# A decoder layer on one Trainium2 core: the products of the conditioning vector with its weights on TensorE instead of VectorE

## The chip, the core and the metric

The kernel runs on one core of one Trainium2 chip. The core has TensorE (PE; its weight loads are shown apart as PEld), VectorE (DVE), ScalarE (ACT), GpSimd (POOL) and SyncE (SP), which here issues nearly all DMA transfers. The metric is the time of one execution on the device in microseconds (us). Three runs of the kernel before took 1175.67, 1179.12 and 1177.77 us; the median is 1177.77.

## What is computed

One layer over 1024 tokens of width 1024, all in float32. A conditioning vector c gives six vectors of length 1024: three for the mixing half (shift, scale, gate 1), three for the MLP half. They are numbered s = 0 to 5, in the order in which the reference splits them: sh1, sc1, g1, sh2, sc2, g2.

```python
c_act = jax.nn.silu(c)                                  # (1, 1024)
mod = c_act @ w_ada + b_ada                             # w_ada: (1024, 6 * 1024)
sh1, sc1, g1, sh2, sc2, g2 = split(mod, 6)
h = rmsnorm(x, pre_mix_g) * (1 + sc1) + sh1
q, k, v, u = split(h @ w_in)                            # 512, 128, 128, 512 columns
attn = sliding_window_attention(q, k, v, attn_sinks)    # window of 128, ALiBi, sinks
ssm = s5_mixer(u, ...)                                  # 32 groups, 64 complex states each, a scan over the tokens
mixed = concat(rmsnorm(attn, ...), rmsnorm(ssm, ...)) @ w_out
x = x + g1 * rmsnorm(mixed, post_mix_g)
h = rmsnorm(x, pre_mlp_g) * (1 + sc2) + sh2
x = x + g2 * rmsnorm(square(relu(h @ w_mlp_in)) @ w_mlp_out, post_mlp_g)
```

The change concerns the second line alone: a vector of 1024 times a matrix of 1024 x 6144 (24 MB in float32).

## The kernel before

The kernel is written with a framework that orders the instructions of each engine itself, by priorities and its own model of time, and sets all waits. Buffers are slots with a name: a new tile in a slot waits until every reader of the tile before it is done. `pin` (line 124) keeps the DMAs that are given to it in the order of the program. Only in the MLP is TensorE's order written out by hand (from line 1345). Each engine works through its queue in order. SyncE's queue is such a queue too: a load that waits for its slot holds up what is issued behind it.

**The vector c.** `cact` (lines 166 to 169) holds silu(c) as 128 x 8: row p of column q is element 128 q + p. A product of c with a block of w_ada is made in two steps. First DVE multiplies the eight row blocks of w_ada (128 rows each) by the columns of cact and adds them up, eight operations in a chain; this leaves a sum for each partition. Then TensorE adds over the 128 partitions, by a product with a tile of ones. A float32 product takes two records in the trace. The slot names that matter: S0 to S3, S6, S7 and G2S hold loaded weights, G1S the sums, PSUM bank D (one bank) the products.

**Shift and scale 1 (lines 368 to 414).** The loop runs over the eight chunks k of the width. `load_k` (line 130) loads the columns of w_ada for shift and scale of chunk k, as four transfers of 256 KB with rows of 512 bytes, three chunks ahead (lines 368, 369, 376). Two chains of four (line 390 on ACT, line 392 on DVE) make the sums `acc`, one addition joins them, and line 397 adds over the partitions into `aps`; lines 399 and 400 make sh1 and G1 of the chunk. With these `h_step(k, 0)` turns the normalised tokens of the first half (transposes `xt`, line 362) into h, as two parts `h1h` and `h1l`, and `u_step` multiplies them with the weights of u (lines 85 to 87, three products each). Beside it run the parameters of the state space model on GpSimd and DVE (`params0` to `params2`, `f_group`).

**Shift and scale 2, gate 1 (lines 417 to 474, 507).** `ada_acc` (line 419) makes a sum `macc` over a whole vector: eight loads `adm` of 512 KB (128 rows of 4 KB) into the ring of four slots RAWS, and eight operations on DVE, 128 x 1024 each (lines 425 and 427). `mods2` makes shift and scale 2 from two such sums (eight products into `mp` each, line 440). `gate` makes gate 1: it adds the bias in one row (line 453), adds over the partitions and copies to all of them in one product with ones (`gp`, line 459), multiplies by the gain of the norm (line 460) and copies the result into slot G1S (line 461), where it stays until the output projection. These steps are taken by `bg_steps`, between the steps of the tokens' second half (lines 479 to 490).

**The scan.** When all of u is there, it is transposed (`ut`, line 498) and multiplied by F (`vp`, line 503); then DVE runs the scan over chunks of tokens (tiles `st`, `Vs`, `qw`, lines 510 to 544), which needs slots G2S and S7 of the ring, and a correction (lines 594 to 608). Beside it run the q, k and v projections (line 617 on; six column blocks m, each with loads `wr`, splits into two parts `whi` on ACT and `wlo` on DVE, and products `pq`), and tables on GpSimd (`Gs`, line 564). The product `kp` (line 575) is the one place where four small products stand side by side in the column groups of the array.

**Output projection (lines 952 to 1004).** For each of eight token tiles j: products `po` (lines 943 to 946), evictions `mix` (lines 948, 950), the residual with gate 1 (`mix` times `macc`, line 967), norm, transposes `x2t` and h of the MLP. Two steps of gate 5 are taken ahead of each tile from the second on (line 993), with a single slot S0 for the loads; the finished gate 5 is stored to DRAM (`g2d`, line 1004) and read again at the end of the MLP (line 1314).

**MLP (line 1005 on).** Products on TensorE, from about 480 us to the end; the change leaves it as it is, but for the name of the DRAM tile that line 1314 reads.

Of the kernel before, what the change touches and what calls it, by code (L numbers as in the profile page):

```python
# [16 lines left out]
P = 128  # L17
D = 1024          # model width
S = 1024          # sequence
NT = 8            # token tiles: tile j holds the tokens 8c + j, c = 0..127  # L20
KC = 8            # 128-row chunks of the model width
FF = 4096
NF = FF // P
G = 32            # SSM groups
CI = 16           # channels of a group
NST = 64          # complex states of a group
W = 512           # attention / SSM width
# [6 lines left out]
def tile_hymba(ctx: ExitStack, tc: tile.TileContext, x, c, w_ada, b_ada, pre_mix_g, w_in,  # L34
# [48 lines left out]
    def mm3(ps, lh, ll, rh, rl, first, last):  # L83
        """ps += l.T @ r of float32 operands given as exact sums of float32r parts."""
        T.matmul(ps, lh, rh, start=first, stop=False)  # L85
        T.matmul(ps, lh, rl, start=False, stop=False)  # L86
        T.matmul(ps, ll, rh, start=False, stop=last)  # L87
# [6 lines left out]
    # ---------------------------------------------------------------- small loads  # L94
    vrow = slot("G2S", [P, P], F32, "vrow")
# [55 lines left out]
    sgn = ct([P, 2], F32, "sgn")      # column 0: +1 | -1, column 1: -1 | +1  # L151
# [17 lines left out]
    tt(V, cact, cact, cT, MUL)  # L169
    vps = ps("C", "vps")  # L170
# [9 lines left out]
    # ---------------------------------------------------------------- SSM parameters  # L180
    # state layout: partitions 0..63 real parts, 64..127 imaginary parts of the 64 states.
# [3 lines left out]
    def params0():  # L185
# [3 lines left out]
        # |a| = exp(v) = (1 + tanh(v/2)) / (1 - tanh(v/2))  # L189
# [4 lines left out]
        V.tensor_scalar(pb[:, 3], lam[:, 1], dtc[:, 0:1], None, op0=MUL)      # angle  # L194
# [16 lines left out]
    def params1():  # L211
        pk = prm[:, 8:16].rearrange("p (o h) n -> p o h n", o=4)  # ar, ai, fr, fi, for both halves
# [8 lines left out]
        # f = (a - 1) / lambda  # L221
# [15 lines left out]
    # ---------------------------------------------------------------- pre-mix norm  # L237
# [24 lines left out]
    # --------------------------------------------------- more SSM parameters  # L262
# [9 lines left out]
    # powers a^1..a^8 (pw) and A^1..A^16 of A = a^8 (qw)  # L272
# [23 lines left out]
    def params2():  # L296
        # B: Bst = [br; bi], Bsw = [-bi; br];  Bb = f B
# [26 lines left out]
    # F[(s, cin), g, (re|im, p)] = (a^(s+1) Bb) transposed; row block s meets token j = 7 - s.  # L324
    # The states so carry one factor a more, and token i reads them through C a^i.
# [17 lines left out]
    # ------------------------------------------- shift/scale 1, h = norm(x), u projection  # L343
# [4 lines left out]
    acc1 = slot("G1S", [P, 2, 2, 2 * P], F32, "acc1")  # L348
# [21 lines left out]
    for k in range(KC):  # L370
# [12 lines left out]
        aps = ps("D", "aps")  # L383
        accs = [acc1[:, k % 2, q] for q in range(2)]
        for i in range(4):
            for q in range(2):
                src = ad[k][q][:, i].rearrange("p s f -> p (s f)")
                sc = cact[:, 4 * q + i:4 * q + i + 1]
                if i == 0:
                    A.activation(accs[q], src, AF.Copy, scale=sc)  # L390
                else:
                    V.scalar_tensor_tensor(accs[q], src, sc, accs[q], op0=MUL, op1=ADD)
        if k:
            tt(V, accs[0], accs[0], accs[1], ADD)
        for s in range(2):
            for q in range(1 if k else 2):
                T.matmul(aps[:, s:s + 1], accs[q][:, s * P:(s + 1) * P], ones[:, 0:1],
                         start=(q == 0), stop=(q == 1 or k > 0))
# [17 lines left out]
    # ------------------------------------------------ shift/scale 2 and gate 1 (background)  # L416
    w_ada_m = w_ada.rearrange("(q p) (s f) -> q s p f", p=P, s=6)

    def ada_acc(s, tag, raws, ld):
        acc = slot(tag, [P, D], F32, "macc")  # L420
        for q in range(KC):
            ab = slot(raws[q % len(raws)], [P, D], F32, "adm")
            ld(SY.dma_start(ab, w_ada_m[q, s]))
            if q == 0:
                V.tensor_scalar(acc, ab, cact[:, 0:1], None, op0=MUL)
            else:
                V.scalar_tensor_tensor(acc, ab, cact[:, q:q + 1], acc, op0=MUL, op1=ADD)  # L427
            yield acc
# [5 lines left out]
    def mods2():  # L434
        for s in (3, 4):
            for acc in ada_acc(s, "G1S", RAWS, pin):
                yield
            mp = ps("D", "mp")
            for k in range(KC):
                T.matmul(mp[:, k:k + 1], acc[:, k * P:(k + 1) * P], ones[:, 0:1], start=True, stop=True)  # L440
            if s == 3:
                tt(V, sh2, mp[:, 0:KC], bT[:, 24:32], ADD)
            else:
                tt(V, G2, mp[:, 0:KC], bsc[:, 1], ADD)
                tt(V, G2, G2, g_mlp, MUL)
            yield

    def gate(s, tag, gain, raws, tmp_tag, ld):
        for acc in ada_acc(s, tag, raws, ld):
            yield  # L450
# [26 lines left out]
    for j in range(4, 8):  # L477
        norm_x(j)
# [522 lines left out]
    for _ in bg:  # L1001
        pass
# [409 lines left out]
```

## Time and profile before

| | |
|---|---|
| runs | 1175.67, 1177.77, 1179.12 us, median 1177.77 |
| the profiled execution | span 1175.7 us, the only time given for it |
| instructions | 14235 |
| TensorE busy | 1038.2 us (88%) |
| VectorE busy | 1009.9 us (86%) |
| ScalarE busy | 559.6 us (48%) |
| GpSimd busy | 576.4 us (49%) |
| mean granted clock of TensorE | 0.954 |
| moved by DMA | 94.98 MB, mean 81 GB/s |

The span goes from the first to the last instruction of the profiled execution; the fastest of the three runs lies within 0.1 us of it. Busy time is the time in which at least one instruction of an engine runs; an engine can be busy and yet not be what the end waits for. So three kinds of views are read together: windows (how full each engine is in a stage), groups (how often a kind of instruction runs, how long one takes, and what ended the idle time before it) and the chain of waits (followed back from the last instruction, at each step to what released it). Rows name the tile written, then the tiles read: `macc<-adm,cact,macc` is the sum of `ada_acc`. The time of a matmul in a row is from its start to its modelled end, so rows of neighbours overlap; the pace is read from start to start.

### The profile page before, as it was taken

How to read it: one execution, taken by the hardware profiler on the slowest of the kernel's cores; microseconds unless marked ns; L12 is line 12 of the kernel's file. 1: busy time of each engine (PE TensorE's matmuls, PEld its weight loads, DVE VectorE, ACT ScalarE, POOL GpSimd, SP SyncE). 2: the span in 40 equal slices, each digit the busy share in tenths (PEclk: the TensorE clock that was granted, in tenths of full speed). 3: DMA queues.
4: the chain of work that ended last, by engine and by line, in shares of the span. 5: the costliest groups of instructions: out<-in, count | busy, mean ns of one | idle time of the engine just before them, and what ended most of it. 6: DMA issues, size and time to landing. Idle time of an engine off the chain costs nothing.

```text
span 1175.7 us, 14235 instructions
## 1 busy us (share of the span) xinstructions
PE 1038.2 (88%) x4770; PEld 818.3 (70%) x4770; DVE 1009.9 (86%) x1632; ACT 559.6 (48%) x1205; POOL 576.4 (49%) x476
## 2 busy tenths in 40 slices
PE   3879757698988999879999999999999999999795
PEld 2658636584555788667877877787787787778684
DVE  6998999959996656888999998999999999898956
ACT  5563330227555366556445545444545554544431
POOL 5863440612666344434455545544645554554645
PEclk9798978889998999989999999999999999999898
DMA  9956114000016433211210120121021022012135
GB/s 271 268 185 224 57 45 77 18 28 1 10 38 178 155 115 121 76 49 32 72 54 28 63 72 27 46 72 46 27 72 59 23 63 72 28 45 72 39 106 195
DMA packets 88158, 94.98 MB, mean 81 GB/s; under 512 B 21778, under 2 KB 67202, under 8 KB 88068
## 3 DMA queue, kind: packets, MB, share of 16 engines
q1 hardware_dynamic: 87748, 94.04, 26.0%
q8 instruction: 37, 0.61, 0.2%
q14 instruction: 37, 0.30, 0.1%
q10 hardware_dynamic: 240, 0.02, 0.0%
q0 software_dynamic: 96, 0.02, 0.0%
HBM read 83.96 MB, written 8.91 MB: 79 GB/s over the span
## 4 chain that ended last, share of the span: by engine, by line
PE 47%; DVE 33%; ACT 6%; issue 5%; POOL 4%; DMA 4%; SPq 0%; DVEq 0%; POOLq 0%; ACTq 0%
PE fo L85 7%; PE fi L87 6%; PE fi L85 6%; PE fi L86 6%; PE fo L86 6%; PE fo L87 6%; DVE facc L90 4%; DVE st L90 4%; DVE f L90 3%; DVE w L90 3%; DVE Vs L90 2%; DVE macc L427 2%; DVE AB L761 2%; POOL s L90 2%; PE po L943 2%
## 5 line engine op out<-in xcount | busy, mean ns | idle before, releaser
L90 POOL TENSOR_TENSOR facc<-facc,tmpc 128x512 f32<-128x512 f32 x106 | 154.0, 1453 | 200.9 <-ACT tmpc L1262 195.4
L90 DVE TENSOR_TENSOR facc<-facc,fo 128x512 f32<-128x512 f32 x335 | 221.1, 673 | 13.6 <-PE fo L87 13.5
L85 PE MATMUL fo<-ops 128*128 128x512 f32 x264 | 105.8, 401 | 15.7 <-DVE facc L90 15.7
L86 PE MATMUL fo<-ops 128*128 128x512 f32 x264 | 103.4, 392 | 0.0
L87 PE MATMUL fi<-h,w 128*128 128x512 f32 x248 | 97.1, 392 | 7.0 <-DVE w L90 7.0
L87 PE MATMUL fo<-ops 128*128 128x512 f32 x264 | 103.3, 391 | 0.0
L85 PE MATMUL fi<-h,w 128*128 128x512 f32 x248 | 96.8, 390 | 0.0
L86 PE MATMUL fi<-h,w 128*128 128x512 f32 x248 | 96.8, 390 | 0.0
L90 DVE TENSOR_TENSOR w<-w1r,w 128x256 fp32r<-128x256 f32 x169 | 94.8, 569 | 1.1 <-ACT w L1028 1.1
L1028 ACT ACTIVATE ops<-f 128x512 fp32r<-128x512 f32 x66 | 41.5, 628 | 105.7 <-PE fo L86 99.7
L1107 ACT ACTIVATE f<-f 128x512 f32<-128x512 f32 x60 | 37.9, 632 | 103.6 <-DVE f L90 103.4
L1028 ACT ACTIVATE w<-w1r 128x256 fp32r<-128x256 f32 x169 | 68.8, 409 | 34.7 <-PE fi L86 25.3
L90 DVE TENSOR_TENSOR f<-fi,f 128x512 f32<-128x512 f32 x120 | 80.3, 680 | 4.7 <-PE fi L87 4.6
L90 DVE TENSOR_TENSOR ops<-f,ops 128x512 fp32r<-128x512 f32 x66 | 58.0, 878 | 25.3 <-ACT ops L1028 15.3
L90 POOL TENSOR_TENSOR w2r<-w2r,w2r 128x512 f32<-128x512 f32 x35 | 49.4, 1414 | 57.0 <-DMA w2r<-in_w_mlp_out_dram 21.8
L85 PEld LDWEIGHTS fo<-ops 128*128 128x128 f32 x264 | 50.0, 189 | 33.8 <-DVE facc L90 24.3
L90 POOL TENSOR_TENSOR w1r<-w1r 128x256 f32<-128x256 f32 x60 | 66.5, 1118 | 11.1 <-DVE w L90 9.7
L87 PE MATMUL pq<-h1h,wlo 128*128 128x512 f32 x96 | 41.0, 446 | 33.8 <-DVE wlo L90 33.8
L1262 ACT ACTIVATE tmpc<-fo 128x512 f32<-128x512 f32 x106 | 61.7, 582 | 11.0 <-POOL facc L90 8.8
L85 PE MATMUL fo<-h2s 128*128 128x512 f32 x128 | 51.0, 398 | 8.8 <-DVE facc L90 8.8
L87 PEld LDWEIGHTS fi<-h,w 128*128 128x128 f32 x248 | 46.8, 189 | 17.2 <-DVE w L90 7.4
L87 PEld LDWEIGHTS fo<-ops 128*128 128x128 f32 x264 | 49.9, 189 | 10.6
(358 smaller groups left out, 3021.2 us busy)
## 6 DMA issues: line engine op xcount, KB each, us to landing
adm<-in_w_ada_dram SPq DMA_DIRECT2D x32, 512.0 KB, 3.5
w2r<-in_w_mlp_out_dram SPq DMA_DIRECT2D x64, 256.0 KB, 2.8
ad<-in_w_ada_dram SPq DMA_DIRECT2D x32, 256.0 KB, 5.6
w1r<-in_w_mlp_in_dram SPq DMA_DIRECT2D x32, 256.0 KB, 3.4
w1r<-in_w_mlp_in_dram SPq DMA_DIRECT2D x16, 512.0 KB, 3.8
xn<-in_x_dram SPq DMA_DIRECT2D x8, 512.0 KB, 6.1
xin<-in_x_dram SPq DMA_DIRECT2D x8, 512.0 KB, 4.3
xs<-xin SPq DMA_DIRECT2D x8, 512.0 KB, 2.8
```

The lines of the kernel that those rows point to most:

```text
L85: T.matmul(ps, lh, rh, start=first, stop=False)
L86: T.matmul(ps, lh, rl, start=False, stop=False)
L87: T.matmul(ps, ll, rh, start=False, stop=last)
L90: e.tensor_tensor(o, a, b, op=op)
L427: V.scalar_tensor_tensor(acc, ab, cact[:, q:q + 1], acc, op0=MUL, op1=ADD)
L761: V.tensor_scalar(Sb[:, i], Sb[:, i], den[:, i:i + 1], None, op0=MUL)
L943: T.matmul(p_, hd[v][h][:, 0, i, o:o + P], woh[v][:, i, sl], start=i == 0, stop=False)
L1028: A.activation(hi, src, AF.Copy)
L1107: A.activation(o, o, AF.Relu)
L1262: A.activation(tmpc, p_, AF.Copy)
```

## The change

It does five things.

1. The sums over the row blocks move to TensorE. `cact32` holds each column of cact 32 times, as a stationary operand of 128 x 32. A block of 256 columns of w_ada is multiplied by it in eight products, one for each row block q, written to partitions 32 (q % 4) onward: four column groups of the array, two row blocks summed in each. ACT copies the result (128 x 256) to `parts_ada`. A product with `sel`, which is 1 in rows 0, 32, 64 and 96 and 0 elsewhere, adds the four groups.
2. The loop over k uses it for shift and scale 1; the loads there stay as they are.
3. For the other vectors a block is 256 columns in place of 1024, loaded in two transfers of 512 KB with rows of 1 KB. The steps of the background are 12 blocks in place of chains of eight.
4. The bias of a gate is added on TensorE too, out of the loaded rows of b_ada; the gate is made in four pieces, each multiplied by the gain on DVE and stored to DRAM (`gd`). Gate 1 is loaded again into G1S ahead of the output projection.
5. Gate 5 is made behind the q projections m = 0 to 3, with one slot S3 for the loads, in place of in the output projection. The tile with c and the rows of b_ada lies in G1S in place of G2S, and the pieces of the gates in JK.

The functions `ada_acc` and `gate` go. The diff follows without them, and without comments and blank lines (the norm of the token tiles 4 to 7 is also written a little earlier in the program, in the same order relative to the background):

```diff
-    vrow = slot("G2S", [P, P], F32, "vrow")
+    adc = slot("G1S", [P, 1024], F32, "adc")
+    vrow = adc[:, 0:P]
...
+    cact32 = adc[:, 2 * P:4 * P].rearrange("p (k r) -> p k r", k=KC)
+    V.tensor_copy(cact32, bc(cact, 2, 32))
+    sel = adc[:, P:2 * P]
+    V.memset(sel, 0.0)
+    for i in range(4):
+        V.memset(sel[32 * i:32 * i + 1], 1.0)
+    parts_ada = adc[:, 4 * P:8 * P].rearrange("p (e f) -> p e f", e=2)
+    n_ada = [0]
+    def ada_parts(srcs):
+        ap_ = ps("D", "ada")
+        for q in range(KC):
+            c0 = 32 * (q % 4)
+            T.matmul(ap_[c0:c0 + 32, 0:2 * P], cact32[:, q], srcs[q], start=q < 4, stop=q >= 4)
+        n_ada[0] += 1
+        o = parts_ada[:, n_ada[0] % 2]
+        A.activation(o, ap_[:, 0:2 * P], AF.Copy)
+        return o, ap_[:, 2 * P:4 * P]
...
-    acc1 = slot("G1S", [P, 2, 2, 2 * P], F32, "acc1")
...
-        aps = ps("D", "aps")
-        accs = [acc1[:, k % 2, q] for q in range(2)]
-        for i in range(4):
-            for q in range(2):
-                src = ad[k][q][:, i].rearrange("p s f -> p (s f)")
-                sc = cact[:, 4 * q + i:4 * q + i + 1]
-                if i == 0:
-                    A.activation(accs[q], src, AF.Copy, scale=sc)
-                else:
-                    V.scalar_tensor_tensor(accs[q], src, sc, accs[q], op0=MUL, op1=ADD)
-        if k:
-            tt(V, accs[0], accs[0], accs[1], ADD)
-        for s in range(2):
-            for q in range(1 if k else 2):
-                T.matmul(aps[:, s:s + 1], accs[q][:, s * P:(s + 1) * P], ones[:, 0:1],
-                         start=(q == 0), stop=(q == 1 or k > 0))
+        part, aps = ada_parts([ad[k][q // 4][:, q % 4].rearrange("p s f -> p (s f)") for q in range(KC)])
+        for e in range(2):
+            T.matmul(aps[:, e:e + 1], part[:, e * P:(e + 1) * P], sel[:, 0:1], start=True, stop=True)
...
+    w_ada_b = w_ada.rearrange("(q p) (s b f) -> p q s b f", p=P, s=6, f=2 * P)
+    n_raw = [0]
+    def ada_block(s, b, raws):
+        srcs = []
+        for q in range(2):
+            a = slot(raws[n_raw[0] % len(raws)], [P, 4, 2 * P], F32, "adm")
+            n_raw[0] += 1
+            pin(SY.dma_start(a, w_ada_b[:, 4 * q:4 * q + 4, s, b, :]))
+            srcs += [a[:, i] for i in range(4)]
+        return ada_parts(srcs)
...
         for s in (3, 4):
-            for acc in ada_acc(s, "G1S", RAWS, pin):
+            for b in range(4):
+                part, o = ada_block(s, b, RAWS)
+                for e in range(2):
+                    T.matmul(o[:, e:e + 1], part[:, e * P:(e + 1) * P], sel[:, 0:1], start=True, stop=True)
+                ks = slice(2 * b, 2 * b + 2)
+                if s == 3:
+                    tt(V, sh2[:, ks], o[:, 0:2], bT[:, 24 + 2 * b:26 + 2 * b], ADD)
+                else:
+                    tt(V, G2[:, ks], o[:, 0:2], bsc[:, 1, ks], ADD)
+                    tt(V, G2[:, ks], G2[:, ks], g_mlp[:, ks], MUL)
                 yield
...
+    gd = {s: dp.tile([P, D], F32, name=f"gate{s}") for s in (2, 5)}
+    gcols = slot("JK", [P, 2, 2 * P], F32, "gcols")
+    def gate_block(s, b, raws):
+        g = gcols[:, b % 2]
+        sl = slice(2 * P * b, 2 * P * b + 2 * P)
+        pin(SY.dma_start(g, (post_mix_g if s == 2 else post_mlp_g)[0, sl].partition_broadcast(P)))
+        part, o = ada_block(s, b, raws)
+        T.matmul(o, sel, part, start=True, stop=False)
+        for e in range(2):
+            r = 64 + 8 * s + 2 * b + e
+            T.matmul(o[:, e * P:(e + 1) * P], ident[64:112, r:r + 1].broadcast_to([48, P]), vrow[64:112],
+                     start=False, stop=e == 1)
+        tt(V, g, o, g, MUL)
+        pin(SY.dma_start(gd[s][:, sl], g))
     def background():
         yield from mods2()
-        yield from gate(2, "G1S", post_mix_g, RAWS, "S3", pin)
+        for b in range(4):
+            gate_block(2, b, RAWS)
+            yield
...
     for k in range(KC):
         h_step(k, 1)
...
-        bg_steps(2)
+        bg_steps(1)
...
-            bg_steps(4)
+            bg_steps(1)
...
-    g1p = gates[2]
...
             A.activation(o, pq[h].rearrange("p (j n l) -> p j n l", j=4, n=8), AF.Copy)
+        if m in (0, 1, 2, 3):
+            gate_block(5, m, ("S3",))
...
+    junk = slot("JK", [P, D], BF16, "junk")
+    g1p = slot("G1S", [P, D], F32, "g1p")
+    SY.dma_start(g1p, gd[2])
     po_half(0, 1)
...
-    bg = gate(5, "G2S", post_mlp_g, ("S0",), "S2", lambda i: i)
     for j in range(NT):
-        for _ in range(2 if j else 0):
-            next(bg, None)
...
-    for _ in bg:
-        pass
-    g2d = dp.tile([P, D], F32, name="g2d")
-    SY.dma_start(g2d, gates[5])
...
-        SY.dma_start(g2p, g2d)
+        SY.dma_start(g2p, gd[5])
```

More of the change, by code (lines that the diff above doesn't have):

```diff
@@ L414, in tile_hymba @@
             f_group(k - 4)
[L417 to L428, printed above, removed]
+    for j in range(4, 8):
+        norm_x(j)
+    w_ada_b = w_ada.rearrange("(q p) (s b f) -> p q s b f", p=P, s=6, f=2 * P)
[8 more added lines that the diff above has]
+        return ada_parts(srcs)
     G2 = ct([P, KC], F32, "G2")
@@ L435, in mods2 @@
         for s in (3, 4):
-            for acc in ada_acc(s, "G1S", RAWS, pin):
-                yield
[L438 to L450, printed above, removed]
-        brow = slot(tmp_tag, [1, D], F32, "brow")
-        ld(SY.dma_start(brow, b_ada[:, s * D:(s + 1) * D]))
-        tt(V, acc[0:1], acc[0:1], brow, ADD)
-        gb = slot(tmp_tag, [P, D], F32, "gb")
-        ld(SY.dma_start(gb, gain[0].partition_broadcast(P)))
-        for h in range(2):
-            gp = ps("D", "gp")
-            sl = slice(h * 512, h * 512 + 512)
-            T.matmul(gp, ones, acc[:, sl], start=True, stop=True)
-            tt(V, gb[:, sl], gp, gb[:, sl], MUL)
-        V.tensor_copy(acc, gb)
-        gates[s] = acc
@@ L464, in tile_hymba @@
-    gates = {}
+            for b in range(4):
[8 more added lines that the diff above has]
+                    tt(V, G2[:, ks], G2[:, ks], g_mlp[:, ks], MUL)
+                yield
@@ L474, in bg_steps @@
             next(bg, None)
-    for j in range(4, 8):
-        norm_x(j)
     for k in range(KC):
```

## The prediction

> **What bounds the kernel now.** I read the windows of 30 us first, to see which engine is full in which stage. Columns: length, then busy us (instructions) of PE, PEld, DVE, ACT and POOL, PE clock, DMA share, GB/s.
>
> ```profile
> core 0: us, PE busy (x) PEld busy (x) DVE busy (x) ACT busy (x) POOL busy (x), PEclk, DMA share, GB/s
> 0.00:30.00 30.00, 11.30 (x42) 8.20 (x42) 19.24 (x56) 15.78 (x29) 16.59 (x34) 1.00 0.94 271
> 30.00:60.00 30.00, 26.44 (x101) 20.18 (x101) 29.82 (x53) 16.27 (x30) 24.88 (x30) 0.77 0.97 257
> 60.00:90.00 30.00, 22.72 (x119) 17.75 (x120) 27.10 (x34) 18.62 (x33) 20.98 (x19) 1.00 0.59 194
> 90.00:120.00 30.00, 27.31 (x158) 24.43 (x157) 24.79 (x25) 12.17 (x22) 8.76 (x6) 0.89 0.71 233
> ...
> 210.00:240.00 30.00, 17.62 (x84) 14.49 (x83) 29.12 (x45) 5.17 (x11) 19.42 (x12) 0.82 0.08 18
> ...
> 360.00:390.00 30.00, 28.29 (x139) 21.11 (x138) 16.23 (x25) 11.26 (x25) 16.84 (x10) 1.00 0.43 127
> 390.00:420.00 30.00, 27.30 (x121) 22.52 (x121) 19.80 (x21) 12.80 (x27) 13.78 (x14) 0.94 0.50 163
> ```
>
> VectorE is full or nearly so from 30 to 240. In the first 60 us the DMA engines are full too. From 360 on PE leads. Next, the share of the sums alone: first the instructions on acc (columns PE, PEld, DVE, ACT, clock, DMA), summed over 0 to 150, then those on macc (PE, PEld, DVE, POOL).
>
> ```profile
> sum 150.00, PE 6.35 PEld 5.80 DVE 36.02 ACT 7.93; mean PE 1.27 PEld 1.16 DVE 7.20 ACT 1.59
> ```
>
> ```profile
> 60.00:90.00 30.00, 0.00 (x0) 0.00 (x0) 10.75 (x8) 0.00 (x0) 1.00 0.59 194
> 90.00:120.00 30.00, 4.89 (x32) 4.91 (x32) 19.69 (x15) 0.00 (x0) 0.89 0.71 233
> 120.00:150.00 30.00, 2.15 (x4) 0.67 (x4) 4.58 (x4) 0.00 (x0) 0.89 0.07 30
> ...
> 360.00:390.00 30.00, 0.00 (x0) 0.00 (x0) 6.33 (x5) 0.00 (x0) 1.00 0.43 127
> 390.00:420.00 30.00, 0.00 (x0) 0.00 (x0) 5.89 (x4) 7.24 (x3) 0.94 0.50 163
> ```
>
> So 36.0 + 35.0 = 71 us of DVE work lie ahead of 150, of the 101 us that DVE is busy up to 120 and a little behind it. Whether they set the end is read from the chain of waits, cut at three places (start, length, what):
>
> ```profile
> 15.12 0.50 ACT acc L390
> ...
> 107.50 1.28 DVE macc L427
> ...
> 108.85 3.04 PE mp L440 x16
> 111.89 5.75 PE ut L498 x32
> 117.63 7.15 PE vp L503 x64
> ...
> 126.78 2.06 DVE st L90
> ...
> 383.26 3.56 DMA adm<-in_w_ada_dram
> ...
> 388.47 1.42 DVE mix L950 x2
> ```
>
> The reader sees three stages. The **front**: sums on DVE hold back the transposes and products ut and vp, and the scan (st) starts at 126.8. The **scan and q/k/v stage**, 126.8 to about 240, on DVE (29.12 of 30 in the row of 210). The **output projection**, where gate 5 loads through one slot: its sum waits in DVE's queue for a load of 3.56 us, with the eviction of po (mix L950) queued behind it.
>
> **The change, part by part: the front.** What goes from DVE is the 71 us, less the small operations that stay. What comes is on PE; its nearest row is the product kp, in four column groups already (128 rows, 16 columns each, 128 moving):
>
> ```profile
> 160.76 0.39 PE L86 MATMUL pq<-h1l,whi 128*128 128x512 f32 x1
> 160.98 0.39 PE L87 MATMUL pq<-h1h,wlo 128*128 128x512 f32 x1
> 161.30 0.63 PE L575 MATMUL kp<-Gs,s 128*16 128x128 f32 x16
> 161.86 0.50 PE L85 MATMUL pq<-h1h,whi 128*128 128x512 f32 x1
> ```
>
> Eight fp32 matmuls (two records each) take 161.30 to 161.86, 0.56 us. Columns alone: a full fp32 product of 512 columns takes 0.86 us (gp, below), so 16 records of 128 take 8 x 0.215 = 1.72 us one behind the other and 0.43 us four abreast; 0.13 us is the coming and going. A block of the change has 8 matmuls of 256 columns: 0.86 + 0.13 = **0.98 us**. Behind it come products with a single moving column (as mp), or for the gates one of 256 columns and two of 128:
>
> ```profile
> 92.23 1.84 PE L440 MATMUL mp<-ones,macc 128*128 128x1 f32 x16
> 93.93 0.64 PE L340 MATMUL fps<-ident,s 128*128 128x128 f32 x4
> ```
>
> ```profile
> 429.50 0.86 PE gp L459 x2
> ```
>
> 16 records of mp start 1.70 us ahead of the next, so four take 0.43; a gate block has 0.43 + 0.43 instead. Ahead of the scan lie 20 blocks: 8 for shift/scale 1, 8 for shift/scale 2, 4 for gate 1: 20 x 0.98 + 16 x 0.43 + 4 x 0.86 = **29.9 us on PE**, in place of the 6.35 + 4.89 us of aps and mp. So I ask what PE needs in all before the scan, at full clock. The u products, three kinds of this many records, step by 0.22 to 0.23 us (pq above is the same shape); the transposes xt and fps take 0.35 us for four:
>
> ```profile
> L85 PE MATMUL u<-wuh,h1h 128*128 128x512 f32 x64 | 29.6, 462 | 0.3 <-ACT h1h L365 0.3
> ```
>
> ```profile
> 83.11 0.60 PE L362 MATMUL xt<-ident,xn 128*128 128x128 f32 x4
> 83.46 0.47 PE L87 MATMUL u<-wuh,h1l 128*128 128x512 f32 x1
> ```
>
> 192 x 0.226 = 43.4 for u; 64 + 32 records, 24 x 0.35 = 8.4 for xt and fps; 5.75 for ut, 7.15 for vp; about 1 for the rest; 29.9 added: 95.6 us. The first block can start at about 15, where ACT now starts on the first columns (chain, 15.12). PE without any gap would reach the scan at 15 + 95.6 = 110.6. It will not be without gaps; the row of 90 to 120 shows 27.31 of 30, 91%, in a stretch where PE has enough to do, and I take that: 15 + 95.6 / 0.91 = **120.1 in place of 126.8, a gain of 6.7 us**. PE is late next, not DVE.
>
> The cover is thinner than it looks. The same sum for now is 43.4 + 8.4 + 5.75 + 7.15 + 68 records of aps and mp x 0.106 = 7.2, + 1 = 72.9 us in 109.8 (15 to the end of vp at 124.8): 66%. Of the 36.9 us that PE has free the change takes 29.9 - 7.2 = 22.7. If the clock stays at 0.77 for 30 us as now, 7 us go, and 3 more in the row of 0.89: about 130, a loss of some 3. On the other side DMA: 30 x (0.94 + 0.97 + 0.59 + 0.71) = 96.3 us of full work up to 120. The 24 large loads change from rows of 4 KB to rows of 1 KB; of the two rows below, the second has 1 KB rows, so 3.8 / 3.5 on some 39 us adds 3:
>
> ```profile
> adm<-in_w_ada_dram SPq DMA_DIRECT2D x32, 512.0 KB, 3.5
> ...
> w1r<-in_w_mlp_in_dram SPq DMA_DIRECT2D x16, 512.0 KB, 3.8
> ```
>
> The last block so lands no earlier than about 101; its own 2 us, ut and vp bring 116. The front's bounds are 116 and 130, and 111 if DMA too had some room left.
>
> The eviction on ACT of a block is 128x256, like the ACTIVATE of acc that goes (7.93 us for 16, 0.50 each): 20 come, 16 go, nothing on balance, as ACT is busy half of the time. The one PSUM bank D passes a block on only after PE, ACT, PE and DVE, an estimate of 0.98 + 0.5 + 0.43 + 0.4 = 2.3 us with two small operations on DVE; 20 blocks have 105 us, so no bound. The vector c's tile no longer lies in G2S, so the third load of w_ada waits less: nothing, DMA is full.
>
> One rule speaks against the change. The Trainium skill (TensorEngine Tiling (Array Packing), Key Properties) says that changing the tiling mode drains TensorE, so each block would pay at its start and its end. The rows above show 0.32 where 0.22 is usual at the start of kp; the whole coming and going is within the 0.13. Were a drain the full tail of a product, 0.39 - 0.22 = 0.17 twice, a block would be 0.21 dearer and the front some 4.6 us later; by that rule the time would be 1172, and the trace bears it out only in part.
>
> **Scan and q/k/v stage.** Out go two products and a copy of gate 1 on DVE; in come four products of gate 5, 128x256 each, and its four blocks, each with two loads through the one slot S3.
>
> ```profile
> 137.16 0.68 DVE L90 TENSOR_TENSOR gb<-gp,gb 128x512 f32<-128x512 f32 x1
> ...
> 152.01 0.67 DVE L461 COPY macc<-gb 128x1024 f32<-128x1024 f32 x1
> ```
>
> 2 x 0.68 + 0.67 = 2.0 out, 4 x 0.4 = 1.6 in (the row halved, a little over): -0.4. On PE 4 x 1.84 = 7.4 us come, and PE waits here for the splits of the weights:
>
> ```profile
> PE pq L87 <- DVE wlo L90: 33.8, 5, 10.6
> ```
>
> So they are covered, unless DVE waits in turn. Its products of gate 5 stand in its queue ahead of scan steps, and behind two loads, PE and ACT. Where DVE was as full (60 to 126) it waited for such loads only briefly:
>
> ```profile
> DVE macc L427 <- DMA adm<-in_w_ada_dram: 2.0, 2, 1.5
> ```
>
> 24 loads cost 2.0 us there; I take **+1.0 us** for 8 loads, between 0 and a load a block. SyncE: 8 loads of 512 KB, and 4 loads and 4 stores of 128 KB for gains and gates, go past the loads of the q/k/v weights and of T in its queue; what they can cost is that same wait, of PE or DVE.
>
> **Output projection.** The DVE queue loses twelve operations and their waits; PE loses the four records of gp. Waits of 355 to 412:
>
> ```profile
> DVE macc L427 <- DMA adm<-in_w_ada_dram: 14.9, 7, 3.9
> ...
> PE x2t L915 <- DVE mix L973: 2.7, 1, 2.7
> ```
>
> PE is the bound (27.30 of 30), so DVE's 14.9 us are worth only what PE waits behind them: 2.7 us, as the first tile's residual comes earlier, plus 2 x 0.86 of gp: **4.4 us**. The bounds are 0, if the weights of w_out keep PE waiting all the same, and 6.1 if the 30 - 28.29 = 1.7 us that PE is idle from 360 to 390 go too. Gate 1's way through DRAM ends with a load of 512 KB (such a one takes 3.5 us, above), issued ahead of the stage's first product and needed only behind the first tile's four: nothing, and one load if that cover is gone. The MLP behind is untouched and moves as a whole.
>
> **The sum** against the profiled execution: 1175.7 - 6.7 - 0.4 + 1.0 - 4.4 = 1165.2. The median of the runs, 1177.77, is 2.1 above this span; the predicted time is **1167.3 us**.
>
> **Rivals.** (a) *Loads and PE run close*: the front at 111 to 116, the projection at its bound: -11 to -16 and -6 give 1156 to 1162. For it: DMA's share of 0.59 and 0.71 from 60 to 120, which leaves it room to run ahead; against: four engines in a ring on one bank. (b) *PE takes over the bound without a gain*: cold clock or drains bring the scan to 126.8 again; only the projection gains: 1175.7 + 0.6 - 4.4 + 2.1 = 1174.0. For it: the clock of 0.77 and a PE share that must rise from 66 to 91%. (c) *Gate 5's loads stop the scan* (the slower side): with one slot, the second load of a block starts only when four matmuls have read the first; PE reaches these behind pq, which waits up to 10.6 us for DVE, and DVE's own product stands behind both. At a full load (3.8 us) a block: +15.2 - 1.0, so 1181.5; from 2.9 us a block (11.5 / 4) the gain is gone. Against: 2.0 us for 24 loads where DVE was full. (d) *The column groups do not run abreast* with 32 columns and sums in place: a block takes 8 x 0.43 = 3.4 us, 49 us more ahead of the scan, and the time would be 1220. Against: kp's 0.56.
>
> **Chances.** Forecast 0.47, (a) 0.15, (b) 0.20, (c) 0.14, (d) 0.04. The range is 1158 to 1183: it leaves out (d) and the far end of (a), and holds (b) and (c) and both bounds of the front. A measurement here tells 0.3%, 3.5 us, from no change. Faster (below 1174.2): the forecast, (a) and half of (b), less 0.03 for the forecast's late end: 0.69. Same: that 0.03, the other half of (b) and 0.02 of (c): 0.15. Slower: the rest of (c) and (d): 0.16.
>
> **What would show it.** Right: the scan's first st at 117 to 123; DVE under 20 of 30 from 30 to 90; PE over 27; blocks of 16 records in about 1 us; no wait of DVE for adm from 360 to 410, with mix L950 2 to 5 us nearer to its product. Wrong: kp-like groups over 1.5 us, PEclk under 0.8 for more than one window from 30 to 110, DVE waits over 2 us on gate products from 125 to 245, or PE waits on ad loads in place of those on acc.

## The result, and the profile after

| | before | after |
|---|---|---|
| median (range) of 4 runs each on one chip | 1176.72 us (1175.12 to 1179.12) | 1217.12 us (1216.80 to 1219.06) |
| ratio, 95% interval | | 1.0338 [1.0312, 1.0365] |
| span of the profiled execution | 1175.7 us | 1215.1 us |
| mean granted clock of TensorE | 0.954 | 0.95 |

The changed kernel is 40 us slower: outside of the predicted range, and on the other side. Its windows of 30 us, columns as in the prediction:

```profile
60.00:90.00 30.00, 28.35 (x190) 21.64 (x193) 15.86 (x28) 19.59 (x37) 15.51 (x14) 1.00 0.50 158
90.00:120.00 30.00, 29.68 (x246) 24.20 (x246) 1.73 (x8) 13.32 (x25) 1.78 (x2) 1.00 0.44 145
120.00:150.00 30.00, 29.72 (x165) 22.62 (x158) 4.79 (x14) 7.56 (x20) 7.07 (x4) 1.00 0.24 67
150.00:180.00 30.00, 29.89 (x151) 21.64 (x150) 3.71 (x10) 6.46 (x16) 0.00 (x0) 1.00 0.43 119
180.00:210.00 30.00, 24.49 (x142) 17.42 (x141) 22.30 (x48) 4.56 (x11) 8.62 (x5) 0.93 0.46 136
210.00:240.00 30.00, 12.13 (x110) 6.55 (x110) 29.51 (x52) 8.11 (x19) 13.01 (x7) 0.61 0.26 84
```

VectorE, full before the change, is busy 1.73, 4.79 and 3.71 of 30 from 90 to 180. It isn't that it has nothing to do: the scan and its correction, which took 115 us before the change (126.7 to 242.0), stand still. TensorE is full meanwhile, and from 210 on the two change places: VectorE full, TensorE 12.13 of 30. The q/k/v products on TensorE and the scan on VectorE, which ran side by side before the change, now run almost one after the other (products `pq` from 121.2 to 201.2, the scan from 187.6 on). The next rows are groups by tile (line, engine, operation, count: shortest, median and longest in ns, first and last start in us): the products `vp`, which are the scan's input, and the scan's first kind of operation.

```profile
L515 PE MATMUL vp<-U,F x64: 275/275/377, 110.8 to 120.7; 128*128 128x128 f32 x64
```

```profile
L90 DVE TENSOR_TENSOR st<-Vs,qw x45: 560/579/2949, 187.6 to 271.3; 64x256 f32<-64x256 f32 x30, 128x256 f32<-128x256 f32 x15
```

The input is there at 121, where 124.8 was before; the scan starts at 187.6 in place of 126.7. What it waits for isn't data. Its table `qw` lies in slot G2S and its scratch `st` in S7, and these are the last two slots of the ring out of which gate 1's blocks load (lines 521 and 528). The timeline of TensorE shows the end of each such block, its product with `sel` at line 470:

```profile
144.18 0.59 PE L470 MATMUL ada<-adc 128*128 128x256 f32 x2
...
160.77 0.59 PE L470 MATMUL ada<-adc 128*128 128x256 f32 x2
...
175.14 0.59 PE L470 MATMUL ada<-adc 128*128 128x256 f32 x2
...
188.90 0.59 PE L470 MATMUL ada<-adc 128*128 128x256 f32 x2
```

One block in 15 us. The eight products of the last one stand in two rows, four each; the second four are the last to read G2S and end at 187.01. VectorE writes `qw` at 187.08:

```profile
185.14 0.64 PE L189 MATMUL ada<-adm,adc 128*32 128x256 f32 x8
...
186.37 0.64 PE L189 MATMUL ada<-adm,adc 128*32 128x256 f32 x8
```

```profile
187.08 0.19 DVE L522 COPY qw<-pw 128x64 f32<-128x64 f32 x1 [9.58 <-DMA wr<-in_w_in_dram]
```

In this row the profile infers that a load of q/k/v weights ended VectorE's 9.58 us of idle time; experiment 1 decides between that and the slot. SyncE's timeline shows why a block takes 15 us:

```profile
145.95 0.34 SPq L476 DMA_DIRECT2D gate<-gcols  x1
146.34 0.43 SPq L468 DMA_DIRECT2D gcols<-in_post_mix_g_dram  x1
146.87 0.95 SPq L439 DMA_DIRECT2D adm<-in_w_ada_dram  x2
149.84 3.15 SPq L635 DMA_DIRECT2D wr<-in_w_in_dram  x4
162.55 0.34 SPq L476 DMA_DIRECT2D gate<-gcols  x1
162.93 0.43 SPq L468 DMA_DIRECT2D gcols<-in_post_mix_g_dram  x1
163.46 0.95 SPq L439 DMA_DIRECT2D adm<-in_w_ada_dram  x2
```

Each block's gate is stored (L476) before the next block's weights are asked for (L439), since both are pinned; and a store is issued only when VectorE has multiplied (the products end at 145.92 and 162.51, the stores are issued at 145.95 and 162.55). The block's three steps on TensorE and VectorE each stand in a queue behind q/k/v products and splits. So four blocks take turns with themselves. Of the 61 us that the scan loses, 41 arrive at the MLP: its first `fi<-h,w` product, with which the output projection's stage is taken to end here and below (a few others of the MLP come up to 11 us sooner), starts at 517.3 in place of 475.8. Attention scores that need no scan are done ahead of its end (the first at 227.2, before the change at 257.4), which may hide part of it.

### The profile page after: what moved, and what is told of

The parts are those of the page before. It is cut to its first block, busy times and chain, and to the rows that moved or that the text cites. A ratio compares the mean times of both kernels' runs of the same rounds, so it can differ in the third digit from the quotient of the medians.

```text
span 1215.1 us, 15028 instructions
## 1 busy us (share of the span) xinstructions
PE 1070.1 (88%) x5190; PEld 830.6 (68%) x5190; DVE 913.4 (75%) x1560; ACT 564.4 (46%) x1214; POOL 559.3 (46%) x476
## 4 chain that ended last, share of the span: by engine, by line
PE 40%; DVE 11%; ACT 3%; issue 2%; DMA 1%; POOL 0%; POOLq 0%; DVEq 0%; SPq 0%; ACTq 0%
PE fo L85 7%; PE fi L87 7%; PE fi L85 7%; PE fi L86 7%; PE fo L86 6%; PE fo L87 6%; DVE facc L90 4%; DVE f L90 3%; DVE w L90 2%; DVE xo L1347 1%; ACT ops L1037 1%; ACT tmpc L1271 1%; DVE h2s L90 0%; ACT h2s L1037 0%; DVE ops L90 0%
## 5 line engine op out<-in xcount | busy, mean ns | idle before, releaser
L90 DVE TENSOR_TENSOR w<-w1r,w 128x256 fp32r<-128x256 f32 x169 | 91.3, 549 | 1.9 <-ACT w L1037 1.9
L1037 ACT ACTIVATE ops<-f 128x512 fp32r<-128x512 f32 x66 | 41.5, 628 | 105.8 <-PE fo L86 99.9
L90 POOL TENSOR_TENSOR s<-s,pw 128x512 f32<-128x512 f32 (+1 forms) x20 | 27.4, 1375 | 83.1 <-DVE qw L90 66.3
```

The lines of the kernel that those rows point to most:

```text
L90: e.tensor_tensor(o, a, b, op=op)
L1037: A.activation(hi, src, AF.Copy)
```

## Experiments

All times are medians; "ratio" is to the kernel before, run on the same chip. "Gate 1 through S3" and so on are edits of the changed kernel unless another base is named.

**1. Slots.** Edit:

```diff
-            gate_block(2, b, RAWS)
+            gate_block(2, b, ("S3",))
```

> Gate 1's blocks load through S3 alone, so that S7 and G2S are free for the scan after the last block of shift/scale 2. Slots (my theory: the scan is late because its tables and its scratch lie in the slots that the last block of gate 1 reads): first st at about 132 in place of 187.6, just behind the last such block (129.8 in the changed kernel); of 61 us at the scan 41 arrived at the MLP, so two thirds of 55 come back: 1217 - 37 = 1180 us. TensorE's queue (rival: the scan's own inputs, or TensorE full of q/k/v products, hold everything): first st after 170, the time 1205 to 1220. Gate 5 in the q/k/v stage or the column products themselves (second rival): the scan starts at 132 but the time stays above 1200.

Measured: 1198.84 us, ratio 1.0165 [1.0133, 1.0198]; first st at 132.5, last m (the end of the scan's correction) at 242.0, as before the change. The slots are what held the scan, and not the scan's input or a load of q/k/v weights; but only 18 of the 37 us came back.

**2. Stores.** Edit:

```diff
-        pin(SY.dma_start(gd[s][:, sl], g))
+        A.dma_start(gd[s][:, sl], g)
```

> The stores of the gates go to ScalarE's queue and no longer stand between the loads of two gate blocks in SyncE's pinned order; the slots are as in the changed kernel. If that store makes the blocks of gate 1 come one at a time: the loads of the second to fourth block are issued before 135 in place of 146 to 178, the blocks follow each other in about 6 us in place of 15, first st at 150 to 160, and two thirds of some 30 us come back: about 1197 us. If TensorE's order makes them late (q/k/v products put ahead of them in its queue): loads early, blocks still 12 us or more apart, first st after 178, 1210 to 1217 us.

Measured: 1210.03 us, ratio 1.0258 [1.0225, 1.0290]; first st at 167.5. In its timeline of TensorE the ends of gate 1's blocks now are:

```profile
143.79 0.59 PE L470 MATMUL ada<-adc 128*128 128x256 f32 x2
...
153.61 0.59 PE L470 MATMUL ada<-adc 128*128 128x256 f32 x2
...
162.26 0.59 PE L470 MATMUL ada<-adc 128*128 128x256 f32 x2
...
171.72 0.59 PE L470 MATMUL ada<-adc 128*128 128x256 f32 x2
```

9.3 us apart in place of 15: the store in the queue was a good third of it. The 6 us that I expected were not reached, so something else holds the blocks too. One such thing is the tile for the gains and gates, which has two halves: the gains of a block can be loaded only when the gate of the block before the last is stored out of the same half, and the weights are pinned behind the gains. SyncE's waits from 118 to 190 (what waited, total us, times, longest):

```profile
SPq L468 <- DMA gate<-gcols: 22.1, 4, 11.5
```

The first two gates are stored at 145.58 and 155.39 (issue on ScalarE's queue), the gains of the third and fourth block are asked for at 149.16 and 158.91.

**3. TensorE's order.** Edit: no q/k/v product ahead of the last product of gate 1 (`ins` is the first of the three products of a q/k/v step, `bgpe` the last product of each gate block; the dependency sets an order on the engine and no wait). First alone, then with the stores of experiment 2.

```diff
+                if m == 4:
+                    tc.add_manual_dep(ins.ins, bgpe[3].ins.name,
+                                      mybir.DependencyInfo(mybir.DependencyClass.NoSync, mybir.DependencyReason.DATA),
+                                      reason="gate 1 first")
```

> On TensorE no q/k/v product may stand ahead of the last product of gate 1; slots and stores are as in the changed kernel. If the q/k/v products in TensorE's queue make the blocks late: a block of gate 1 takes 8 to 9 us (gain and weights 4.3 to 5, product, eviction, second product, product on VectorE, store) in place of 15, first st at 160 to 168, and with q/k/v products some 40 us later, which the scan covers, 1200 to 1208 us. If the order counts for nothing: first st after 180 and 1217 us, or later by the products that were moved behind.

> Slots as in the changed kernel, gate stores on ScalarE's queue, and no q/k/v product ahead of gate 1's last product on TensorE. If TensorE's queue is what is left between two blocks once the store is gone (9.3 us apart with the stores edit alone): blocks 5 to 6 us apart, the bound of two loads, the first at 128 in place of 144, first st at 148 to 155 in place of 167.5, and 1198 to 1203 us in place of 1210. If it isn't: blocks 9 us apart, first st at 167 or later, and 1210 or more.

Measured: alone 1220.78 us, ratio 1.0350 [1.0318, 1.0383], no gain where I had expected 1200 to 1208 if the order counts; only its time is used here. With the stores 1216.77 us, ratio 1.0320 [1.0291, 1.0349]. First st at 149.9 is inside of what I expected if TensorE's queue were the rest, the time is not: 7 us slower than the stores alone. The rows of `pq`, first of experiment 2, then of this one, show what it cost:

```profile
L85 PE MATMUL pq<-h1h,whi x96: 387/389/796, 120.8 to 226.4; 128*128 128x512 f32 x96
```

```profile
L85 PE MATMUL pq<-h1h,whi x96: 388/389/793, 152.1 to 274.9; 128*128 128x512 f32 x96
```

The scan gained 18 us, the q/k/v products lost 48, and the attention needs both. My "which the scan covers" was wrong.

**4. Slots and stores.**

> Both the slots of the first edit and the stores of the second. If the slots alone hold the scan, the stores are worth nothing once the scan is free: within 5 us of the slots edit alone, about 1180. If the late blocks of gate 1 and 5 also cost something by themselves (ScalarE and VectorE waits behind them), it is over 5 us faster than that: 1170 or under.

Measured: 1196.84 us, ratio 1.0150 [1.0123, 1.0177], 2 us under the slots alone: as expected if the scan no longer waits for gate 1, but far from the 1180 that I expected of either. Some 20 us are still lost behind the scan.

**5. Bank D and gate 5.** With the slots edit the scan's stage ends where it did, but the products `yp` of the SSM's output, which use banks C and D by turns, come late. Rows of `yp`, before the change and in experiment 1:

```profile
L645 PE MATMUL yp<-T,U x64: 270/275/377, 209.2 to 262.4; 128*128 128x128 f32 x64
```

```profile
L658 PE MATMUL yp<-T,U x64: 270/275/580, 222.9 to 329.1; 128*128 128x128 f32 x64
```

Three edits ask whether gate 5's blocks, the last of which holds bank D until 306, are the reason. With the slots edit, (a) gate 5 goes back to the output projection, or (b) stays and `yp` and the transposes `zt` leave bank D; (c) is (a) without the slots edit.

```diff
-        if m in (0, 1, 2, 3):
-            gate_block(5, m, ("S3",))
...
+        if 1 <= j <= 4:
+            gate_block(5, j - 1, ("S0",), gcol5, lambda i: i)
```

```diff
-        yp = psR("CD", "yp")
+        yp = psR("CB", "yp")
...
-            tp = psR("CD", "zt")
+            tp = psR("CB", "zt")
```

> The slots edit of the first experiment, and gate 5's four blocks moved from the q/k/v loop back to the output projection (through S0, gain columns in S2, gate 1 loaded into G2S). With the slots edit alone the scan stage ended where it does before the change (last m at 242.0 in both), and yet the last SSM product came at 329.1 in place of 262.4 and the MLP 24 us late. If gate 5's blocks, the last at 306 and in the bank D that half of the SSM products use, hold them back: last yp near 265, first product of the MLP near 476, 1199 - 23 = 1176 us or a little under. If they don't (rival: order of scores and SSM products by itself, or gate 1's blocks): last yp over 310 and 1190 or more.

> The slots edit of the first experiment, with gate 5 left in the q/k/v loop, but the SSM products and the transposes behind them use banks C and B in place of C and D. If bank D, held by gate 5's blocks, is what makes the SSM products late: last yp before 280 and 1178 to 1184 us. If slot S3 (from which the weights of the output projection load next) or the queues of gate 5's blocks make the loss: yp early, but the first product po still near 375 and the time within 5 us of 1199. If neither: yp late as before.

> Gate 5 in the output projection as in the run before the last, but gate 1's blocks through the four slots of the changed kernel. If the two costs are apart and add up: the scan starts at 187 as in the changed kernel, and the time is 1217 - 23 = 1194 us or, as the late scan hides part of gate 5's cost, up to 1210. If the late scan alone is the whole loss: 1217.

Measured: (a) 1187.05 us, ratio 1.0091 [1.0059, 1.0123], last yp 274.2; (b) 1187.22 us, ratio 1.0081 [1.0057, 1.0105]; its row of `yp`:

```profile
L658 PE MATMUL yp<-T,U x64: 270/275/377, 222.4 to 260.7; 128*128 128x128 f32 x64
```

So bank D made the SSM's output late, and it is worth 10 to 12 us (by the ratios and by the times), less than I had expected in (a) and (b): 1176, and 1178 to 1184. (c) missed: 1233.70 us, ratio 1.0482 [1.0448, 1.0517], slower than the changed kernel. In the output projection gate 5's blocks cost as well. From the first `po` to that first `fi<-h,w` it takes 117.1 us before the change (358.7 to 475.8), 122.5 after it (394.8 to 517.3), 129.3 in (a) (359.1 to 488.4) and 137.7 in (c) (397.6 to 535.3). With the slots edit the old place of gate 5 (a) and the new one without bank D (b) come to the same time; with the late scan the old place is the slower one (c). So what cost time in the new place was bank D.

**6. Earlier still.** (a) of experiment 5, and the last two blocks of scale 2 through S3 and S6.

```diff
-                part, o = ada_block(s, b, RAWS)
+                part, o = ada_block(s, b, RAWS if (s, b) < (4, 2) else ("S3", "S6"))
```

> As the first of this set, and the last two blocks of shift/scale 2 load through S3 and S6, not S7 and G2S. If only those slots hold the scan behind the last product vp (121.7): first st at 122 to 125 in place of 132, 5 to 7 us off the time of the first of this set, about 1170, under the kernel before. If TensorE, 29.7 of 30 busy there, sets the scan in another way: first st unchanged within 3 us, and the same time.

Measured: first st at 121.5, as expected, but 1198.83 us, ratio 1.0179 [1.0154, 1.0204], where I had expected 1170: 12 us slower than without it. Waits from 118 to 255 (engine, line, what it waited for, total us, times, longest):

```profile
PE pq L87 <- DVE wlo L90: 17.9, 2, 12.9
...
PE ada L189 <- DVE G L90: 14.3, 2, 9.0
...
PE ada L189 <- DMA adm<-in_w_ada_dram: 6.1, 1, 6.1
```

The blocks now fall into the scan. VectorE's small operation on G (scale 2), which empties bank D, stands in its queue behind scan steps; the next block's product waits for the bank, 9.0 us once (it starts at 138.81, the operation on G at 138.57), and the q/k/v products wait behind that in TensorE's queue (last pq 252.8, 243.3 in (a), where TensorE has no such wait for G).

**7. All three mended.** Slots, stores, and `yp` and `zt` off bank D.

> The slots edit, the SSM products off bank D, and the gate stores on ScalarE's queue together. If the pinned stores still cost time once slots and bank are out of the way: 5 us or more under the 1187 of slots and bank, that is 1182 or less. If not: 1187 within 3 us, and what is left of the loss lies elsewhere (TensorE's longer front, the order of the attention's and the GLU's work).

Measured: 1178.86 us, ratio 1.0003 [0.9988, 1.0018]. With the scan and bank D free, the pinned stores cost 8 us, or 9 by the ratios. The three together account for the whole loss: 40 us back to parity. The share of each depends on the order in which they are taken: the stores are worth 2 us in experiment 4 and 8 here. And the front gives no gain, since st is at 132.2.

**8. One part alone.** From the kernel before: only shift and scale 1 go to TensorE; the rest stays on VectorE. Then shift and scale 2 too, in the changed kernel's blocks, through the same ring.

```diff
+    cact32 = S5[:, 1536:1792].rearrange("p (k r) -> p k r", k=KC)
...
+        part, aps = ada_parts([ad[k][q // 4][:, q % 4].rearrange("p s f -> p (s f)") for q in range(KC)])
```

> One part of the change alone: only the eight products of shift/scale 1 go to TensorE (its c columns in a free part of the tile s5); shift/scale 2, gate 1 and gate 5 are running sums on VectorE, placed as before the change. It takes 36 us of sums off VectorE ahead of the scan and adds 8 blocks, some 11 us, to TensorE, less the 6.35 us of the old products. If the front was held by VectorE, as I had argued, and the loss of the change lies in the blocks of shift/scale 2 and of the gates: first st at 110 to 118 in place of 126.7, later stages as before, 1163 to 1172 us. If the front is bound by the loads (96 us of full DMA work up to 120) or by TensorE: first st at 122 to 127, 1174 to 1179. If the order in which the later stages then are put eats any gain: first st early, time at 1176 or above.

> As the run before it, with the eight blocks of shift/scale 2 on TensorE too (in the same four slots), and both gates still running sums on VectorE. TensorE gets 8 x 1.4 = 11 us more ahead of the scan, where it was full (29.7 of 30) in the changed kernel; VectorE loses 10 us more of sums. If TensorE is the front's bound by then: first st 4 to 10 us later than in the run before it, and slower by about that much less what the attention hides. If VectorE or the loads still bound it: the same time within 3 us or faster.

Measured: shift and scale 1 alone, 1170.41 us, ratio 0.9933 [0.9912, 0.9954]; it and the kernel of experiment 10 are the only ones faster than the kernel before. The time is as expected if VectorE held the front, the scan's start (120.6) is not: it lies between the 110 to 118 of that reading and the 122 to 127 of the other. Shift and scale 2 as well: 1190.47 us, ratio 1.0107 [1.0085, 1.0130]. Their first rows of `st`:

```profile
L90 DVE TENSOR_TENSOR st<-Vs,qw x45: 572/587/2326, 120.6 to 196.4; 64x256 f32<-64x256 f32 x30, 128x256 f32<-128x256 f32 x15
```

```profile
L90 DVE TENSOR_TENSOR st<-Vs,qw x45: 567/586/2956, 145.6 to 217.3; 64x256 f32<-64x256 f32 x30, 128x256 f32<-128x256 f32 x15
```

25 us between them, for an estimated 11 us of work on TensorE. SyncE's loads `adm` (start, length of the group, count), again in that order:

```profile
61.16 2.13 SPq L425 DMA_DIRECT2D adm<-in_w_ada_dram  x4
...
67.40 44.07 SPq L425 DMA_DIRECT2D adm<-in_w_ada_dram  x20
```

```profile
61.71 2.29 SPq L446 DMA_DIRECT2D adm<-in_w_ada_dram  x4
...
69.41 44.55 SPq L446 DMA_DIRECT2D adm<-in_w_ada_dram  x12
...
119.82 18.19 SPq L425 DMA_DIRECT2D adm<-in_w_ada_dram  x8
```

In 44 us VectorE takes 20 loads out of the ring, TensorE 12. Gate 1's eight loads, all issued by 111.5 in the first kernel, begin at 119.8 in the second, though DMA is less than half busy there (share 0.44 from 90 to 120). The blocks run at 68.7, 78.9 to 80.0, 89.8, 99.9 and so on: they seem to wait for their place in TensorE's queue, which the next experiment changes.

**9. The place in the queue.** The u products of chunk k (second half of the tokens) stand behind block k of shift and scale 2 (`adapes` holds the last product of each block), in the second kernel of experiment 8 and in that of experiment 7.

```diff
+        if j >= 4:
+            tc.add_manual_dep(ins.ins, adapes[KC + k].ins.name,
+                              mybir.DependencyInfo(mybir.DependencyClass.NoSync, mybir.DependencyReason.DATA),
+                              reason="shift/scale 2 by turns with u")
```

> As the kernel with the products of shift/scale 1 and 2 on TensorE and both gates on VectorE (1190.5 us, first st 145.6), but the u products of chunk k of the second half of the tokens stand behind block k of shift/scale 2 in TensorE's queue, so that a block runs every 4 us from 69 on and not every 6 to 10 us up to 130. If the place of these blocks in TensorE's queue kept the ring of four slots taken, and so the loads for gate 1 late (issued from 119.8 there, 105 at the latest when shift/scale 2 is on VectorE): last block before 108, loads of gate 1 issued from 105, first st at 119 to 125, 1169 to 1176 us. If TensorE simply has too much to do ahead of the scan, or waits for the loads instead: u, ut and vp end 5 us or more later than 121, first st after 127, 1178 or more.

> The whole change with all that was found: gate 1 through S3, SSM products off bank D, gate stores on ScalarE's queue (1178.9 us, first st 132.2), and the same order of u products and blocks of shift/scale 2. If the blocks' place in the queue was what still kept the scan 6 us later than before the change: first st at 121 to 124, and 1169 to 1174 us. If not: first st at 130 or later, or a late u, and 1178 or more.

Measured: the first 1178.14 us, ratio 1.0004 [0.9988, 1.0020], first st at 126.5; its loads and its u products:

```profile
62.05 2.30 SPq L454 DMA_DIRECT2D adm<-in_w_ada_dram  x4
...
69.76 30.58 SPq L454 DMA_DIRECT2D adm<-in_w_ada_dram  x12
...
104.11 12.29 SPq L433 DMA_DIRECT2D adm<-in_w_ada_dram  x8
```

```profile
L85 PE MATMUL u<-wuh,h1h x64: 387/395/795, 23.1 to 112.0; 128*128 128x512 f32 x64
```

Both halves hold in part. The blocks' place was worth 19 us of st (145.6 to 126.5) and 12 us of the time. But u now ends at 112.0 in place of 104.2, and 6 us to the kernel with shift and scale 1 alone (120.6) stay. TensorE's own work for the eight blocks would fit that (it is busy 27.92 of 30 us from 90 to 120); it was not shown apart. The whole change with this order missed: first st at 128.6, and 1194.68 us, ratio 1.0133 [1.0106, 1.0160]. Behind the scan its q/k/v products end at 260.0 (246.3 in experiment 7) and wait 33.0 us for VectorE's splits from 130 to 240 (19.8 there); why the framework's order comes out so wasn't followed further.

**10. TensorE's last steps.** From the first kernel of experiment 8: the small products of scale 2 behind `vp`, gate 1's sum in S5.

```diff
-            mp = ps("D", "mp")
...
+    mods2_tail(4, held[0], vpi)
```

> As the kernel with the products of shift/scale 1 alone on TensorE (1170.4 us, first st 120.6), but the 16 small products of scale 2 on its running sum, ahead of which TensorE there waits 2.34 us and which take 1.95 us in front of ut, stand behind vp; gate 1's sum lies in S5 and goes to G1S when it is done. If TensorE's last steps ahead of the scan set its start: first st 3 to 4 us earlier, at 116.5 to 117.5, and 1167 us. If VectorE's sums for gate 1 or their loads (the last issued at 111) are as late: first st 119 to 121 and the same time.

Measured: 1170.74 us, ratio 0.9947 [0.9924, 0.9970]. `vp` starts 5.4 us earlier, at 105.9, the scan only 2.2, at 118.4, between my two readings, and the time is the same. Here `vp` ends at 113.2, but the last of VectorE's sums for gate 1 runs from 115.42 to 116.70, behind a load (the last is issued at 111), and `qw` and `st` follow at 117.88 and 118.40. In experiment 8 the two ends were close, 118.7 for `vp` and 118.0 for the sums. So the front has no single bound left: behind TensorE come VectorE's sums and their loads.

## Why the prediction was wrong

**The view of the bound** (VectorE ahead of the scan) was right, with TensorE and the loads close behind: taking 36 of its 71 us away brings st only from 126.7 to 120.6, and 7.8 us in the end (experiment 8).

**The cost of a block on TensorE** was right: 0.98 us predicted, 1.00 measured from start to start.

```profile
34.54 1.07 PE L189 MATMUL ada<-ad,adc 128*32 128x256 f32 x16
35.54 0.66 PE L385 MATMUL xt<-ident,xn 128*128 128x128 f32 x4
```

By this row rival (d) falls. By the Trainium skill (TensorEngine Tiling (Array Packing), Key Properties) a change of the tiling mode drains TensorE; here a block with its coming and going takes 1.00 us, 0.86 of it columns, so no drain beyond the 0.13 us that the prediction already had from `kp` shows.

**The step that failed** is "15 + 95.6 / 0.91 = **120.1 in place of 126.8**". TensorE did reach the end of vp at 121.0, 0.9 us after my 120.1, but the scan started at 187.6: I took the end of vp for the start of the scan. (Even before the change the two lie 2 us apart, 124.8 and 126.8, so that the gain by this sum was 4.7 us and not 6.7.) Before the change the slots of the ring were emptied by VectorE, the engine that runs the scan next; it could not come to the scan with them still full. After it they are emptied by TensorE, which runs ahead with other work. "20 blocks have 105 us, so no bound" was the same error: it added up a block's four steps as 2.3 us without the queues that each step stands in (15 us from block to block), and without the pinned store and load between two blocks, which I had priced for gate 5 alone, as a short wait.

That 121.0 came so near to 120.1 was luck. The 95.6 us hold 20 blocks, and only 15 had started by then: the last of shift and scale 2 starts at 129.79, those of gate 1 from 138.24 on. By the prediction's own prices the five are 8.8 us. Even so TensorE was busy for 97.1 of the 106 us from 15 to 121 (92%), so the sum had the other work some 10 us too small: the u products, put at 43.4 us, are busy for 53.73 in that stretch (columns PE, PEld, ACT).

```profile
15.00:121.00 106.00, 53.73 (x192) 36.80 (x192) 4.46 (x8) 0.98 0.70 201
```

**Gate 5 in the q/k/v stage.** I took +1.0 us. It cost 10 to 12 by bank D (experiment 5), and the stores, gate 1's among them, 8 more once slots and bank were free (experiment 7). The rival (c), that its blocks stop the scan's stage, had the right kind of mechanism (an in-order queue behind a block that waits), at the wrong place: experiment 6 shows it in the scan, the changed kernel showed it in gate 1, whose blocks I had priced without asking who takes their slots next.

**The output projection.** -4.4 us was wrong too: it takes 122.5 us after, 117.1 before. The first eviction by VectorE comes 38.5 us after the first po (433.3 and 394.8) where it came after 29.8 (388.5 and 358.7), and not 2 to 5 us sooner. The waits of VectorE for `adm` are gone, as predicted; from 355 to 425 it waits for the halves of w_out, which are loaded and split in that stretch (most of these loads are issued from 388.47 on, before the change from 334.55), and TensorE waits too:

```profile
DVE wol L875 <- ACT woh L869: 8.0, 4, 3.7
...
PE rp L852 <- POOL sss L90: 7.3, 1, 7.3
```

The granted clock differs as well: 0.82 in those 38.5 us, 1.00 in the 29.8 us before the change. Which of these makes the difference was not shown.

**What followed as said:** DVE under 20 of 30 up to 90, TensorE over 27 from 60 to 180 (25.97 from 30 to 60), the clock at 0.94 or more up to 180. The sign that would have told is in my own list, the scan's first st at 117 to 123.

## What to carry to other kernels

When work moves from one engine to another, follow the buffers and not only the work: ask which engine now frees each slot and bank, what stands ahead of the freeing instruction in that engine's queue, and who takes the slot next. A loop of load, product, eviction, product and store that is pinned in one queue runs one round at a time, however short its steps. And moving the part whose buffers nobody else waits for (here shift and scale 1) may hold all of the gain.

## What I had not expected of the hardware

In these traces a store that waits for its data on SyncE's queue holds the loads behind it (issues at 145.95 to 146.87 and 162.55 to 163.46, above). Eight stores of 0.34 us (rows of L476) are 2.7 us of issue time, yet moving them to ScalarE's queue, out of the pinned order, was worth 8.4 us (1187.22 to 1178.86; ratios 1.0081 and 1.0003). The Trainium skill (Trainium Kernel Development and Optimization, Key Constraints) says that issuing DMAs from several engines only saves the sequencer's issue time. The gain measured here is three times that issue time: the wait of a store in the queue counts too, though what each later stage gained by it was not followed up (the first `po` comes at 359.3 in place of 364.6).
